# Earlier attention scores for three pairs of heads, and the gates' Strassen unit written out in another order

## The chip, the cores and the metric

The kernel runs on one core of a Trainium2 chip. The metric is device time in microseconds of one execution. The core has a TensorE (PE, matrix products into eight PSUM banks), a VectorE (DVE), a ScalarE (ACT), a GpSimd engine (POOL) and a SyncE queue (SP) that issues DMAs; POOL and ACT can issue DMAs too. Each engine takes its instructions in one fixed order and stops at the first one whose inputs or output buffer are not ready.

## The reference

Two layers, each a half-step feed-forward block, a mixer and another half-step feed-forward block on 256 tokens of width 1024, each followed by a layer norm. The change lies in the mixer:

```
z = x @ w_in;  u, v, q, k, val, gates = split(z)
h_a = chunked_sgu(gelu(u), gelu(v))            # per 128-token chunk, lower triangular
q, k = rope(q), rope(k)
a = softmax(q0 k0) - lam * softmax(q1 k1)      # 8 heads, two score maps each, causal
h_b = rmsnorm(a @ val) * (1 - lam_init)
g = sigmoid(gates + gate_b)                    # [tokens, 2 branches, 1024]
m = g[0] * (h_a @ w_branch[0]) + g[1] * (h_b @ w_branch[1]);  out = m @ w_out
```

All inputs and outputs are float32. Each operand is split into a high and a low part (`whi`/`wlo` for weights), and a product is made as hi·hi + lo·hi + hi·lo.

## The kernel before

TensorE's order is written out by hand: the program's text is the order of the matrix products. The other engines' orders come from a list scheduler at build time, which places each instruction by a priority (`step()` raises it with every chunk of weights) and by its own estimate of when it becomes ready. Two tools bend that. `behind(ins)`, which is `tc.issue_after(ins)`, adds an edge "not before `ins`" to those instructions of its block that stand on the engine of `ins`; instructions of other engines in the block get no edge. `beside(task, delay)` sets a side task aside: a generator whose pieces are put into the text when a counter of product work (`beat`) has advanced by the delay, and whose `yield`s are further delays. A beat is one piece of a gate column's chunk (8 products with `whi` and 8 half-size ones with `wlo`), some 2.8 us.

The mixer of a layer runs in this order on TensorE: values; eight projections for q and k (`rope`, four pairs of heads); four chunks of gate columns and two of u (`gemm_a2`: 16 products with `whi`, L296, then 16 half-size ones with `wlo`, L303), and between these the seven products of the gates' Strassen unit (`gates_by_rows`, products in `product`, L377); the v projection (L284); two more chunks of u; then the branches, of which the first (`branch_rows(1, hb)`, L284) reads `hb`, the result of attention.

Attention is a side task for each pair of heads (`attend`). The four pairs are counted from one here. A pair's way is: scores on TensorE (L1018), maximum and exponentials (DVE L1030, ACT L1032), difference of the two maps (DVE L1041), transposition through POOL (L217), a DMA on SP (L221) and ACT (L1066), the product with the values on TensorE (L1072 and L1074), copy and squares on ACT (L1077, L1082), an inverse root in 16 small steps on POOL (`rsqrt4`, L269 to L277), scaling (ACT L1091), a second transposition (POOL L217, SP L221, DVE L230), and the two parts of `hb` (ACT L1106, DVE L1108).

PSUM has four banks with the tag `main` and four with the tag `side`. A pair's scores take four side banks, its product with the values one. The unit keeps one main bank from its first to its last product, so the gate columns turn round in the other three; a column's bank is free when DVE has added its two halves (`gz`, L306), for which ACT first copies one half (`r`, L304).

The unit's summed weights are made in place: a raw tile is split (`pieces`, ACT L248 and DVE L250), and then POOL adds the next weights to it by an accumulating DMA (`gather`, L354). Before, a gather after a product was itself a side task one beat later (`add_in`).

Of the kernel before, what the change touches and what calls it, by code (L numbers as in the profile page):

```python
# [17 lines left out]
ALU = mybir.AluOpType  # L18
# [19 lines left out]
HC = CH // 2  # L38
# [17 lines left out]
def trunk(ctx, tc, x, xT, w13a, w13b, w2, wb, wqk, wu, wg, wgr, wbr, wbrr, wo, gateb, gatebr, sgug, sgub, sguwT, sgubias, lam, diffg,  # L56
          lng, lnb, lngT, lnbT, cosT, sinT, out):
    nc = tc.nc
    V, A, G, PE = nc.vector, nc.scalar, nc.gpsimd, nc.tensor
# [15 lines left out]
    def name(s):  # L75
        serial[0] += 1
        return f"{s}_{serial[0]}"

    def bank():
        return psum.tile([P, 512], F32, tag="main", name=name("bank"))  # L80
# [4 lines left out]
    def slots(s, n, dtype=F32):  # L85

        return [act.tile([P, 512], dtype, tag="slot", name=name(s)) for _ in range((n + 1) // 2)]
# [22 lines left out]
    def step():  # L110
        chunk[0] += 1
        tc.cur_priority = chunk[0] * STEP
# [12 lines left out]
    def beat(w):  # L125

        clock[0] += w
        for task in list(tasks):
            if task[0] <= clock[0]:
                turn(task)  # L130

    def turn(task):
        try:
            task[0] = clock[0] + next(task[1])
        except StopIteration:
            tasks.remove(task)

    def beside(task, delay):
        tasks.append([clock[0] + delay, task])
# [9 lines left out]
    line = [None, None, False]  # L149

    def inline(eng, ins):
        if line[2]:
            line[eng is V] = ins
        return ins

    def behind(ins):

        return tc.issue_after(ins) if ins is not None else nullcontext()

    def fetch(src, width=CH, raw=None):  # L160

        step()
        if raw is None:
            raw = raw_pool.tile([P, CH], F32, tag="raw", name=name("raw"))
        for g in gate:
            g[0] -= 1
        while len(gate) > 1 and gate[1][0] < 0:
            gate.pop(0)
        with behind(gate[0][1] if gate and gate[0][0] < 0 else None):
            if isinstance(raw, list):  # L170
                for j, v in enumerate(raw):
                    loaded[0] = nc.sync.dma_start(v, src[:, j * HC : (j + 1) * HC]).ins
            else:
                loaded[0] = nc.sync.dma_start(raw[:, :width], src).ins
        return raw
# [70 lines left out]
    def split(hi, lo, src, eng=V, after=(None, None)):  # L246
        with behind(after[0]):
            a = A.activation(hi, src, AF.Copy).ins  # L248
        with behind(after[1]):
            return a, eng.tensor_tensor(out=lo, in0=src, in1=hi.bitcast(F32), op=ALU.subtract).ins  # L250
# [97 lines left out]
    def halved(v):  # L348
        return v if isinstance(v, list) else [v[:, o : o + HC] for o in range(0, CH, HC)]

    def gather(raw, more):
        step()
        for j, v in enumerate(halved(raw)):
            G.dma_start(v, more[:, j * HC : (j + 1) * HC], accum_op=ALU.add)  # L354
        return raw

    def plus(raw, more):
# [2 lines left out]
                inline(V, V.tensor_tensor(out=v, in0=v, in1=m, op=ALU.add).ins)  # L360
        return raw

    def pieces(raw):
        out = []
        for v in halved(raw):
            hi = hi_pool.tile([P, HC], F32R, tag="hi", name=name("whi"))
            lo = lo_pool.tile([P, HC], F32R, tag="lo", name=name("wlo"))
            for eng, ins in zip((A, V), split(hi, lo, v, after=line[:2])):
                inline(eng, ins)
            out.append((hi, lo))  # L370
        return out

    def product(ps, x, w, start, stop):
        for k in range(4):
            hi, lo = (v[:, k % 2 * 512 : k % 2 * 512 + 512] for v in w[k // 2])
            for n, (y, o) in enumerate(((hi, 0), (lo, 0), (hi, 1))):
                PE.matmul(ps, x[o](k), y, start=start and k == n == 0, stop=stop and k == 3 and n == 2,  # L377
                          skip_group_check=True)
            beat(0.25)

    def gemm_seven(src, xh, xl, sums, ln, done):

# [42 lines left out]

        r1 = fetch(w11)
        p1 = pieces(r1)
        r2 = fetch(w12, raw=homes(hi_pool, "hi"))
        product(bx, a11, p1, True, False)
        ln.fold(0, 0, bx, ALU.add, True)  # L430
        between()
        p2 = pieces(fetch(w21))
        plus(r1, r2)
        product(q[0][0], a12, p2, False, False)
        gather(r2, w22)
        r3 = fetch(w22, raw=homes(lo_pool, "lo"))
        between()
# [151 lines left out]
    def bc_load(src, after):  # L589
        t = res.tile([P, D], F32, tag="bc", name=name("bc"), bufs=2)  # L590
        V.tensor_copy(t[:, :1], after)
        spread[0] = G.dma_start(t, src.partition_broadcast(P)).ins
        return t
# [376 lines left out]
    def mixer(l, i, norm):  # L970
# [14 lines left out]
        def rope(src, scale):  # L985

            (_, z), = gemm_a2([src], both, lambda m: slots("z", 2)[0], lambda: t512("r"), scale)
            sw, r = t512("swap"), slots("qk", 2)[0]
            for h in range(2):
                nc.sync.dma_start(sw[h::2, :], z[1 - h :: 2, :])  # L990
            r3, z3, s3 = (v.rearrange("p (j t) -> p j t", j=2) for v in (r, z, sw))
            c, s = (v.unsqueeze(1).to_broadcast([P, 2, T]) for v in (cos_t, sin_t))
            V.tensor_tensor(out=r3, in0=z3, in1=c, op=ALU.mult)
            turned_by[0] = G.tensor_tensor(out=s3, in0=s3, in1=s, op=ALU.mult).ins  # L994

            def rest():
                with behind(added[0]):
                    V.tensor_tensor(out=r, in0=r, in1=sw, op=ALU.add)
                yield 0

            beside(rest(), 1.55)
            return r
# [108 lines left out]
        gates, grow, x_sums = [], [], []  # L1111
# [6 lines left out]
        def gates_by_rows():  # L1118

            x11, x12, x22 = (tuple(lambda k, o=o, t=t, h=h: x_cat[h][:, k, o + t * P : o + (t + 1) * P] for o in (0, T))  # L1120
                             for t, h in ((0, 0), (0, 1), (1, 1)))
            (w11, w21), (w12, w22) = ([wgr[l, br, 0][:, o : o + CH] for o in (0, CH)] for br in range(2))
            grow.extend([slots("gr", 2)[0] for _ in range(NT)] for _ in range(2))
            (g00, g10), (g01, g11) = grow

            def add_in(raw, w):
                def task():
                    gather(raw, w)
                    yield 0
                beside(task(), 1)  # L1130
            bias = [gbias[:, br * 512 : (br + 1) * 512] for br in range(2)]

            def sum_up(out, in0, in1, op, end=False):
                added[0] = V.tensor_tensor(out=out, in0=in0, in1=in1, op=op).ins
                if end:
                    emptied[0] = A.activation(out, out, AF.Tanh, scale=0.5).ins

            bx = bank()
            r1 = fetch(w11)
            product(bx, x11, pieces(r1), True, False)  # L1140
            add_in(r1, w12)
            sum_up(g00, bx, bias[0], ALU.add)
            yield
            bq = bank()
            product(bq, x12, pieces(fetch(w21)), True, True)
            sum_up(g00, bq, g00, ALU.add, True)
            yield
            bz = bank()
            product(bz, x_sums[0], pieces(r1), True, False)
            add_in(r1, w22)  # L1150
            sum_up(g11, bz, bias[1], ALU.add)
            yield
            r3 = fetch(w22)
            product(bz, x_sums[3], pieces(r3), False, True)
            add_in(r3, w12)
            sum_up(g01, bz, bias[1], ALU.add)
            yield
            product(bx, x_sums[1], pieces(r1), False, False)
            add_in(r1, w21)
            sum_up(g01, g01, bx, ALU.subtract, True)  # L1160
            yield
            product(bx, x_sums[2], pieces(r3), False, False)
            sum_up(g11, g11, bx, ALU.subtract, True)
            yield
            product(bx, x22, pieces(r1), False, True)
            sum_up(g10, bx, bias[0], ALU.add, True)
            yield

        beside(sums_of_x(), 3.5)
        for hp in range(HEADS // 2):  # L1170
            qT = rope(wqk[l, hp, 0], HD ** -0.5)
            kT = rope(wqk[l, hp, 1], 1.0)
            beside(attend(hp, qT, kT), 4.5 + 2.1 * hp)
            if hp == 1:
                gbias = bc_load(gatebr[l], qT[:, :1])

# [143 lines left out]
    for l in range(DEPTH):  # L1320
        norm = ffn(l, 0, 0, norm)
        norm = mixer(l, 1, norm)
        norm = ffn(l, 1, 2, norm, last=l == DEPTH - 1)
# [87 lines left out]
```

## Time and profile before

| | |
|---|---|
| median of 3 runs | 1215.14 us (1214.31 to 1221.01) |
| the profiled execution | 1212.97 us, span 1211.3 us |
| PE, DVE, ACT, POOL busy | 1185.6, 1042.6, 839.6, 301.1 us |
| granted TensorE clock, mean | 0.993 |
| the first layer's unit and gate columns | 250.4 to 317.9 us |
| the second layer's | 848.6 to 919.0 us |
| start of the branch that reads `hb` | 352.5 and 954.2 us |

In a timeline row the columns are start, duration, engine, line, operation, output and inputs, shapes, count of instructions merged into the row, and in brackets how long the engine had been idle before it and what ended that. Matrix products overlap: a row's duration is longer than its distance to the next, so rates are read from starts. Line numbers are those of the kernel before.

### The profile page before, as it was taken

What the parts mean: (1) busy time and instruction counts of PE and PEld (TensorE: products, weight loads), DVE (VectorE), ACT (ScalarE), POOL (GpSimd) and SP (SyncE); (2) the same over time, 40 slices, a digit from 0 to 9 for tenths busy, and PEclk for the clock granted to TensorE, in tenths of its full rate; (3) what the DMA queues carried; (4) which work ended last, traced back from release to release, by engine and by line L of the source; (5) the groups of instructions that cost most, each with busy time, mean ns of one, the idle gap of its engine ahead of it and who ended that gap; (6) DMA issues with size and microseconds to landing.
All of it is one profiled execution on the core that took longest, in us unless ns stands there. A gap on an engine that the chain in (4) does not pass through costs nothing.

```text
span 1211.3 us, 16711 instructions
## 1 busy us (share of the span) xinstructions
PE 1185.6 (98%) x5753; PEld 994.5 (82%) x5753; DVE 1042.6 (86%) x1596; ACT 839.6 (69%) x1439; POOL 301.1 (25%) x366
## 2 busy tenths in 40 slices
PE   9999999989989999999999999999799899999998
PEld 8888888878878888888888888888688688888887
DVE  6889989988788989889898889889887799898895
ACT  6787667659854676886667976676698456679770
POOL 1013200255430220071020260003554212201610
PEclk9999999999999999999999999999899999999999
DMA  9867967769864668689578689486797655786880
GB/s 351 271 229 236 303 218 273 239 189 272 280 202 160 194 213 270 194 271 274 184 249 278 206 265 283 135 330 187 203 275 248 217 170 169 248 261 198 271 238 35
DMA packets 131637, 281.40 MB, mean 232 GB/s; under 512 B 89264, under 2 KB 90592, under 8 KB 107744
## 3 DMA queue, kind: packets, MB, share of 16 engines
q1 hardware_dynamic: 121680, 246.57, 61.0%
q0 software_dynamic: 9296, 33.10, 12.2%
q8 instruction: 45, 0.74, 0.2%
q10 hardware_dynamic: 576, 0.66, 0.2%
q14 instruction: 40, 0.33, 0.1%
HBM read 254.35 MB, written 1.05 MB: 211 GB/s over the span
## 4 chain that ended last, share of the span: by engine, by line
PE 75%; DVE 8%; ACT 6%; POOL 4%; DMA 4%; issue 3%; SPq 0%; DVEq 0%; ACTq 0%; POOLq 0%
PE bank L284 37%; PE sbank L377 12%; PE bank L411 9%; PE bank L296 6%; PE sbank L411 3%; PE bank L303 3%; DVE wlo L198 2%; DMA swap<-z 2%; PE bank L531 2%; ACT whi L196 1%; ACT pp L1032 1%; DMA raw<-in_wgr 1%; PE bank L377 1%; DVE wlo L250 1%; DMA on<-onT 1%
## 5 line engine op out<-in xcount | busy, mean ns | idle before, releaser
L198 DVE TENSOR_TENSOR wlo<-raw,whi 128x1024 fp32r<-128x1024 f32 (+1 forms) x330 | 358.7, 1114 | 50.2 <-ACT whi L196 42.8
L196 ACT ACTIVATE whi<-raw 128x1024 fp32r<-128x1024 f32 (+1 forms) x334 | 306.4, 946 | 108.0 <-PE bank L284 34.7
L284 PE MATMUL bank<-whi,x 128*128 128x512 f32 x1096 | 344.6, 389 | 0.0
L284 PEld LDWEIGHTS bank<-whi,x 128*128 128x128 f32 x1096 | 205.8, 188 | 42.6
L284 PE MATMUL bank<-wlo,x 128*128 128x512 f32 x548 | 213.2, 389 | 0.0
L250 DVE TENSOR_TENSOR wlo<-raw,whi 128x1024 fp32r<-128x1024 f32 (+1 forms) x151 | 179.8, 1212 | 29.8 <-ACT whi L248 22.8
L248 ACT ACTIVATE whi<-raw 128x1024 fp32r<-128x1024 f32 (+1 forms) x151 | 149.9, 1012 | 61.5 <-DVE raw L360 31.5
L296 PE MATMUL bank<-x,whi 128*128 128x512 f32 x640 | 157.8, 398 | 12.8 <-DVE z L306 9.2
L296 PEld LDWEIGHTS bank<-x,whi 128*128 128x128 f32 x640 | 119.6, 191 | 40.5 <-DVE z L306 10.2
L284 PEld LDWEIGHTS bank<-wlo,x 128*128 128x128 f32 x548 | 102.9, 188 | 21.3
L230 POOL COPY seven<-seven 128x512 uint16<-128x512 uint16 x16 | 67.0, 4248 | 125.1 <-ACT whi L196 81.1
L303 PEld LDWEIGHTS bank<-x,wlo 128*128 128x128 f32 x640 | 82.1, 193 | 3.2
L303 PE MATMUL bank<-x,wlo 128*128 128x256 f32 x640 | 83.4, 285 | 0.0
L411 PE MATMUL bank<-whi,hhi 128*128 128x512 f32 (+1 forms) x182 | 68.2, 374 | 0.0
L411 PE MATMUL bank<-whi,hlo 128*128 128x512 f32 (+1 forms) x182 | 67.9, 373 | 0.0
L411 PE MATMUL bank<-wlo,hhi 128*128 128x512 f32 (+1 forms) x182 | 67.9, 373 | 0.0
L758 POOL COPY nvia<-ntwo 128x256 uint16<-128x256 uint16 x20 | 10.4, 567 | 158.4 <-DMA ntwo<-nvia 132.6
L994 POOL TENSOR_TENSOR swap<-swap,sin_t 128x512 f32<-128x512 f32 x16 | 23.9, 1493 | 99.2 <-DMA swap<-z 90.3
L1032 ACT ACTIVATE pp<-pp,mx 128x256 f32<-128x256 f32 (+1 forms) x64 | 28.2, 442 | 23.4 <-DVE mx L1030 23.4
L304 ACT ACTIVATE r<-bank 128x256 f32<-128x256 f32 x96 | 33.9, 372 | 13.0 <-PE bank L303 12.7
L377 PE MATMUL sbank<-whi,xhs 128*128 128x512 f32 x128 | 42.0, 389 | 0.0
L411 PEld LDWEIGHTS bank<-whi,hlo 128*128 128x128 f32 x182 | 34.3, 188 | 6.1
(303 smaller groups left out, 2294.6 us busy)
## 6 DMA issues: line engine op xcount, KB each, us to landing
raw<-in_w13b SPq DMA_DIRECT2D x68, 1024.0 KB, 6.0
raw<-in_w SPq DMA_DIRECT2D x32, 1024.0 KB, 6.1
raw<-in_wb SPq DMA_DIRECT2D x16, 1024.0 KB, 7.5
raw<-in_wqk SPq DMA_DIRECT2D x16, 1024.0 KB, 7.0
home<-in_w13b SPq DMA_DIRECT2D x16, 512.0 KB, 6.3
raw<-in_w13a SPq DMA_DIRECT2D x8, 1024.0 KB, 4.9
home<-in_w SPq DMA_DIRECT2D x16, 512.0 KB, 4.5
raw<-in_wg SPq DMA_DIRECT2D x8, 1024.0 KB, 5.7
```

The lines of the kernel that those rows point to most:

```text
L196: inline(A, A.activation(h, r, AF.Copy).ins)
L198: low = eng.tensor_tensor(out=w, in0=r, in1=h.bitcast(F32), op=ALU.subtract).ins
L230: eng.tensor_copy(out=o, in_=i)
L248: a = A.activation(hi, src, AF.Copy).ins
L250: return a, eng.tensor_tensor(out=lo, in0=src, in1=hi.bitcast(F32), op=ALU.subtract).ins
L284: PE.matmul(ps, xx, w, start=start and n == 0, stop=stop and n == 2)
L296: PE.matmul(b[-1], hi[:, k * P : (k + 1) * P], xc(k), start=k == 0, stop=False)
L303: PE.matmul(b[n][:, :T], lo[:, k * P : (k + 1) * P], xc(k)[:, :T], start=False, stop=k == KT - 1)
L304: emptied[0] = A.activation(r[:, s], b[n][:, T:], AF.Copy, scale=scale).ins
L377: PE.matmul(ps, x[o](k), y, start=start and k == n == 0, stop=stop and k == 3 and n == 2, skip_group_check=True)
L411: PE.matmul(q[c][t][:, :n] if o == 0 else more[:, :n], x(k, t), y, start=k == 8 and m == 0 and (c, t) != (1, 0) and not o, stop=k == FT - ...
L1032: A.activation(p[:, s], p[:, s], AF.Exp, bias=mx[:, a], scale=-1.0, accum_out=sums[:, a])
```

## The change

In `gates_by_rows` the gathers are no longer side tasks: each stands in the text right behind the product that it follows, inside `behind(m)`, where `m` is that product's last matrix instruction; and four of the `pieces` calls take `m` too. In `attend`'s delays, 4.5, 6.6, 8.7 and 10.8 beats become 4.5, 6.2, 7.25 and 9.25.

```diff
-    def gather(raw, more):
+    def gather(raw, more, after=None):
         step()
         for j, v in enumerate(halved(raw)):
-            G.dma_start(v, more[:, j * HC : (j + 1) * HC], accum_op=ALU.add)
+            with behind(after):
+                G.dma_start(v, more[:, j * HC : (j + 1) * HC], accum_op=ALU.add)
...
-    def pieces(raw):
+    def pieces(raw, after=None):
...
-            for eng, ins in zip((A, V), split(hi, lo, v, after=line[:2])):
+            for eng, ins in zip((A, V), split(hi, lo, v, after=(after, after) if after else line[:2])):
...
-                PE.matmul(ps, x[o](k), y, start=start and k == n == 0, stop=stop and k == 3 and n == 2,
-                          skip_group_check=True)
+                last = PE.matmul(ps, x[o](k), y, start=start and k == n == 0, stop=stop and k == 3 and n == 2,
+                                 skip_group_check=True)
             beat(0.25)
+        return last.ins
...
-            def add_in(raw, w):
-                def task():
-                    gather(raw, w)
-                    yield 0
-                beside(task(), 1)
...
-            product(bx, x11, pieces(r1), True, False)
-            add_in(r1, w12)
+            m = product(bx, x11, pieces(r1), True, False)
+            gather(r1, w12, m)
...
-            product(bz, x_sums[0], pieces(r1), True, False)
-            add_in(r1, w22)
+            m = product(bz, x_sums[0], pieces(r1, m), True, False)
+            gather(r1, w22, m)
...
-            product(bz, x_sums[3], pieces(r3), False, True)
-            add_in(r3, w12)
+            m = product(bz, x_sums[3], pieces(r3), False, True)
+            gather(r3, w12, m)
...
-            product(bx, x_sums[1], pieces(r1), False, False)
-            add_in(r1, w21)
+            m = product(bx, x_sums[1], pieces(r1, m), False, False)
+            gather(r1, w21, m)
...
-            product(bx, x_sums[2], pieces(r3), False, False)
+            m = product(bx, x_sums[2], pieces(r3, m), False, False)
...
-            product(bx, x22, pieces(r1), False, True)
+            product(bx, x22, pieces(r1, m), False, True)
...
-            beside(attend(hp, qT, kT), 4.5 + 2.1 * hp)
+            beside(attend(hp, qT, kT), (4.5, 6.2, 7.25, 9.25)[hp])
```

Here `m` stands on PE, the gather on POOL, the split on ACT and DVE. With the edits of the unit alone, all five engines' orders read as before, row for row; what moves in the built program moves with the four delays. The first pair keeps its place, and so do the second pair's scores; the third and the fourth move.

TensorE in the first layer, at the first pair's product with the values (`sbank_2619`) and the third pair's scores. Before, the scores stood in the gate column that follows, between its `whi` and `wlo` products:

```order
L377 MATMUL bank_2605<-whi_2612,x_1213 128x512
L296 MATMUL bank_2656<-x_1212,whi_2648 128x512 [waits DVE_49]
L296 MATMUL bank_2656<-x_1212,whi_2648 128x512 x3
L296 MATMUL bank_2656<-x_1213,whi_2648 128x512 x4
L296 MATMUL bank_2690<-x_1212,whi_2652 128x512 [waits DVE_49]
L296 MATMUL bank_2690<-x_1212,whi_2652 128x512 x3
L296 MATMUL bank_2690<-x_1213,whi_2652 128x512 x4
L1018 MATMUL sbank_2703<-qk_2346,qk_2285 128x256
```

and in the change (where L1020 is the line of the scores, L1074 and L1076 those of the values, L378 the unit's):

```order
L1074 MATMUL sbank_2619<-val_1699,d_2278 128x128 [waits Pool_49]
L1076 MATMUL sbank_2619<-val_1699,aT_2279 128x128
L1076 MATMUL sbank_2619<-val_1700,aT_2279 128x128
L1020 MATMUL sbank_2639<-qk_2346,qk_2285 128x256
L1020 MATMUL sbank_2640<-qk_2346,qk_2285 128x256
L1020 MATMUL sbank_2639<-qk_2346,qk_2285 128x256
L1020 MATMUL sbank_2640<-qk_2346,qk_2285 128x256
L1020 MATMUL sbank_2645<-qk_2346,qk_2285 128x128
L1020 MATMUL sbank_2646<-qk_2346,qk_2285 128x128 [waits Activation_49]
L1020 MATMUL sbank_2645<-qk_2346,qk_2285 128x128
L1020 MATMUL sbank_2646<-qk_2346,qk_2285 128x128
L378 MATMUL bank_2605<-whi_2608,x_1213 128x512
```

The scores now stand directly behind the product whose side bank their fourth bank, `sbank_2646`, takes over; the wait on ACT in the sixth row of the scores stood in the same row before. The fourth pair's scores move in the same way, out of the fourth gate column into the unit's fourth product just ahead of it.

ACT in the first layer, from the column copy of the chunk before. Before:

```order
L304 ACTIVATE r_2581<-bank_2566 128x256
L1187 ACTIVATE gate_2512<-gz_2582,gbh 128x256 x2
L1077 ACTIVATE on_2626<-sbank_2619 128x512
L1082 ACTIVATE d_2277,ss_2628<-on_2626 128x128 x4
L248 ACTIVATE whi_2863<-raw_2861 128x1024
L248 ACTIVATE whi_2867<-raw_2861 128x1024
L1136 ACTIVATE gr_2514<-gr_2514 128x512
L196 ACTIVATE whi_2886<-raw_2884 128x1024
L196 ACTIVATE whi_2890<-raw_2884 128x1024
L1032 ACTIVATE pp_2715,sums_2700<-pp_2715,mx_2699 128x256 x2
```

and in the change:

```order
L1183 ACTIVATE gate_2512<-gz_2582,gbh 128x256 x2
L1079 ACTIVATE on_2626<-sbank_2619 128x512
L1084 ACTIVATE d_2277,ss_2628<-on_2626 128x128 x4
L1034 ACTIVATE pp_2651,sums_2636<-pp_2651,mx_2635 128x256 x2
L1034 ACTIVATE pp_2656,sums_2636<-pp_2656,mx_2635 128x256 x2
L1034 ACTIVATE pp_2661,sums_2636<-pp_2661,mx_2635 128x128 x2
L1034 ACTIVATE pp_2666,sums_2636<-pp_2666,mx_2635 128x128 x2
L248 ACTIVATE whi_2865<-raw_2863 128x1024
L1132 ACTIVATE gr_2514<-gr_2514 128x512
L248 ACTIVATE whi_2869<-raw_2863 128x1024
L196 ACTIVATE whi_2926<-raw_2924 128x1024
```

The third pair's eight exponentials go ahead of five instructions; the copy `on_2626<-sbank_2619` keeps its place behind the gate column's two.

DVE in the first layer, at the copy `onT` of the fourth pair, from which `hb_1934` and `hb_1935` are made. Before:

```order
L198 TENSOR_TENSOR wlo_3786<-raw_3783,whi_3785 128x1024
L306 TENSOR_TENSOR u_3556<-bank_3567,r_3605 128x256
L230 COPY onT_3481<-on_3358 128x512 x2
L306 TENSOR_TENSOR u_3556<-bank_3596,r_3605 128x256
L261 TENSOR_SCALAR nwa_3683<-nwy_3680,ve_3671 128x1
L198 TENSOR_TENSOR wlo_3790<-raw_3783,whi_3789 128x1024
L1108 SCALAR_TENSOR_TENSOR hb_1934<-onT_3481,dgs,hb_1934 128x256
```

and in the change:

```order
L198 TENSOR_TENSOR wlo_3570<-raw_3563,whi_3569 128x1024
L198 TENSOR_TENSOR wlo_3640<-raw_3637,whi_3639 128x1024
L230 COPY onT_3445<-on_3316 128x512 x2
L198 TENSOR_TENSOR wlo_3644<-raw_3637,whi_3643 128x1024
L1208 BN_STATS vst_3273<-vg_3271 128x6
```

The copy stands 32 rows earlier, ahead of the norm of v, and the two `hb` rows 13 rows earlier, right behind the first half of the third chunk of u.

More of the change, by code (lines that the diff above doesn't have):

```diff
@@ L1144, in gates_by_rows @@
             bq = bank()
-            product(bq, x12, pieces(fetch(w21)), True, True)
+            m = product(bq, x12, pieces(fetch(w21)), True, True)
             sum_up(g00, bq, g00, ALU.add, True)
```

## The prediction

> **What bounds the kernel now.** The page first, since it says which engine a gain has to come from.
>
> ```profile
> span 1211.3 us, 16711 instructions
> PE 1185.6 (98%) x5753; PEld 994.5 (82%) x5753; DVE 1042.6 (86%) x1596; ACT 839.6 (69%) x1439; POOL 301.1 (25%) x366
> ```
>
> TensorE is busy 98% of the span, so a change that adds no product can only win or lose at TensorE's waits. The view of waits on that engine lists them (total, times, longest):
>
> ```profile
> PE bank L296 <- DVE z L306: 9.2, 3, 5.7
> PE bank L284 <- ACT hb L1106: 6.1, 2, 3.0
> PE bank L296 <- DVE gz L306: 3.6, 6, 1.0
> PE bank L284 <- DVE hb L1108: 1.1, 2, 0.7
> PE bank L284 <- DVE u L306: 1.0, 2, 0.8
> ```
>
> The first stands before anything the change moves. The `hb` waits are the fourth pair of heads coming late to the branch; the `gz` waits lie between the unit's products. Their price is more than the idle time, as TensorE's timeline shows, first layer, then second:
>
> ```profile
> 341.02 3.79 PE L296 MATMUL bank<-x,whi 128*128 128x512 f32 x16
> 344.65 2.08 PE L303 MATMUL bank<-x,wlo 128*128 128x256 f32 x16
> ...
> 356.47 0.39 PE L284 MATMUL bank<-whi,hb 128*128 128x512 f32 x1
> 359.90 0.50 PE L284 MATMUL bank<-whi,hb 128*128 128x512 f32 x1 [3.04 <-ACT hb L1106]
> ...
> 367.95 1.05 PE L1244 MATMUL sbank<-wsT,vg 128*128 128x128 f32 x8
> ...
> 958.17 0.39 PE L284 MATMUL bank<-whi,hb 128*128 128x512 f32 x1
> ...
> 969.20 1.05 PE L1244 MATMUL sbank<-wsT,vg 128*128 128x128 f32 x8
> ```
>
> Sixteen undisturbed products go from 341.02 to 344.65, 0.227 us each. From the last product before the wait to L1244 lie 25 such steps (one, six with the fourth pair's `hb`, eighteen more), worth 5.67 us. They took 11.48 and 11.03, so the two `hb` waits cost 5.8 and 5.4 us, 11.2 in all, slow clock behind them included.
>
> Why is `hb` late? PE, ACT, SP and DVE in the first layer, and the landing times of the transposing DMA:
>
> ```profile
> 317.91 0.39 PE L284 MATMUL bank<-whi,x 128*128 128x512 f32 x1
> ...
> 327.43 0.38 PE L1072 MATMUL sbank<-val,d 128*128 128x128 f32 x2
> ```
> ```profile
> 339.42 1.28 ACT L1091 ACTIVATE on<-on,nwy 128x128 f32<-128x128 f32 x4 [3.64 <-POOL nwy L277]
> ```
> ```profile
> 341.95 1.24 SPq L221 DMA_TRANSPOSE on<-onT x1
> ```
> ```profile
> 341.68 2.46 DVE L198 TENSOR_TENSOR wlo<-raw,whi 128x1024 fp32r<-128x1024 f32 x2 [4.64 <-ACT whi L196]
> ...
> 352.01 0.42 DVE L306 TENSOR_TENSOR u<-bank,r 128x256 f32<-128x256 f32 x1
> ...
> 358.47 0.78 DVE L230 COPY onT<-on 128x512 uint16<-128x512 uint16 x2
> ```
> ```profile
> DMA to landing us min/median/max: 4.6/6.6/10.2
> ```
>
> The block lands near 348.6 (341.95 + 6.6), at the latest 352.2, but DVE comes to it at 358.47 without having waited: it stood in DVE's queue. So two things matter, when the fourth pair's chain ends and where its rows stand on DVE.
>
> **The change part by part.** *The unit's edits* cost and bring nothing. Their order edges would tie POOL, ACT and DVE to an instruction of PE, and such an edge binds only an instruction of the same engine; the order of all engines is the same with and without them.
>
> *The fourth pair, sooner.* Its product with the values stood behind 42 products of the v projection ((327.43 - 317.91) / 0.227) and now stands behind 18, which is 5.4 us less, while TensorE will be some 2 us late there (next part): 3.4 us sooner. If the rest of the chain follows, the scaling comes at 336.0, the DMA at 338.5, the block at 345.1, at the latest 348.8. The DVE copy now stands between the two splits of 341.68, so DVE waits there from 342.9 to 345.1, and all behind it comes 2 to 3 us later: `u` at 352.01 becomes 354 to 355, which is when TensorE, 2 us late, first needs it (that cover is thin: each us more is a us of waiting), and the `hb` rows follow `u` directly, four to five us before TensorE wants them. In the second layer the copy stands behind `u` and holds nothing up. Both `hb` waits go: **11.2 us**.
>
> *The third pair, sooner.* Here the change adds a wait. TensorE around the place, first layer:
>
> ```profile
> 265.49 0.47 PE L377 MATMUL bank<-whi,x 128*128 128x512 f32 x1
> ...
> 268.19 3.92 PE L296 MATMUL bank<-x,whi 128*128 128x512 f32 x16 [0.39 <-DVE gz L306]
> 272.05 1.58 PE L1018 MATMUL sbank<-qk,qk 64*128 64x256 f32 x16
> 273.55 2.18 PE L303 MATMUL bank<-x,wlo 128*128 128x256 f32 x16
> ...
> 278.09 0.39 PE L377 MATMUL bank<-whi,xhs 128*128 128x512 f32 x1
> 279.49 3.96 PE L296 MATMUL bank<-x,whi 128*128 128x512 f32 x16 [1.00 <-DVE gz L306]
> ```
>
> The scores took 272.05 to 273.55. They will begin at 265.49, and their sixth row takes the side bank of the first pair's values, which ACT has to copy out first. Five of eight rows (four of 256 columns, one of 128) are three quarters of 1.50 us, so TensorE stops at 265.49 + 1.13 = 266.6. ACT's copy and what it stands behind:
>
> ```profile
> 264.85 2.96 DVE L250 TENSOR_TENSOR wlo<-raw,whi 128x1024 fp32r<-128x1024 f32 x2
> 267.73 0.74 DVE L306 TENSOR_TENSOR gz<-bank,r 128x256 f32<-128x256 f32 x2
> ```
> ```profile
> 268.18 0.91 ACT L1187 ACTIVATE gate<-gz,gbh 128x256 f32<-128x256 f32 x2 [3.02 <-DVE gz L306]
> 268.99 0.58 ACT L1077 ACTIVATE on<-sbank 128x512 f32<-128x512 f32 x1
> ```
>
> The copy follows two gate rows, these follow `gz`, and `gz` follows two weight splits on DVE. None of it depends on a product later than 265.49, so the copy ends at 269.57 as before, and TensorE stands for 269.6 - 266.6 = 3.0 us. Behind it in TensorE's queue wait the rest of the unit's second product and the whole gate column. In the second layer the same rows are these:
>
> ```profile
> 866.60 0.47 PE L377 MATMUL bank<-whi,x 128*128 128x512 f32 x1
> ```
> ```profile
> 870.11 0.57 ACT L1077 ACTIVATE on<-sbank 128x512 f32<-128x512 f32 x1
> ```
>
> 870.7 - (866.6 + 1.1) = 3.0 again: **6.0 us** of standing.
>
> Then the clock. After a stand of the same length the profile shows this:
>
> ```profile
> 258.12 3.25 PE L296 MATMUL bank<-x,whi 128*128 128x512 f32 x8 [3.02 <-DVE z L306]
> 261.17 2.53 PE L303 MATMUL bank<-x,wlo 128*128 128x256 f32 x16
> 263.54 0.40 PE L377 MATMUL bank<-whi,x 128*128 128x512 f32 x1
> ```
>
> Eight products and sixteen half-size ones took 263.54 - 258.12 = 5.42 us; at the rates of 341.02 to 346.56 they take 1.81 + 1.91. The stand cost 1.7 us more in slow products, and the two `hb` waits (11.2, less 6.1 + 1.1 of idle) 2.0 each. I take 1.7 each, **3.4 us**; the bounds are 0 and 2.1.
>
> The Trainium skill (TensorE: Matmul & The Clock Gate, section "What's actually happening") says that the clock is halved after at least one idle window of about 3.4 us, the windows running freely. By that rule a stand of 3.0 us holds no whole window and costs no slow products, and the sum below would be 3.4 us better; the row after 3.02 us of idle speaks against it.
>
> *What TensorE's lateness takes away.* It comes 4 us later to 279.49, while ACT's two copies `r` stay where they were:
>
> ```profile
> 278.61 0.63 ACT L304 ACTIVATE r<-bank 128x256 f32<-128x256 f32 x2
> ```
>
> In the new order ACT does the eight exponentials from 270.8 to 274.6 (3.5 us, as long as before), four splits and a gate row (4.4 us), and these copies at 279.0; DVE, through the difference of the maps and three splits, gives `gz` at 280.6. TensorE arrives near 282, so it does not wait. In the same way the waits at 268.19 and before the fourth column go, and TensorE, 2 us late, no longer waits for `u`. All six `gz` waits and both `u` waits: 3.6 + 1.0 of idle, and each loses 0.17 us more between starts than it shows as idle (279.49 - 278.09 - 0.23 = 1.17 for 1.00), so 4.6 + 1.3 = **5.9 us**; bounds 0 and 5.9.
>
> *The gather that moves.* On POOL the third gather now stands behind the third pair's transposition copies. This is the one that landed slowest, in the chain of waits:
>
> ```profile
> 278.72 12.20 DMA raw<-in_wgr
> ```
>
> I put its issue 2 us later, so landing near 293. By the same walk through ACT's order (exponentials of the fourth pair from 290.7 to 294.2) ACT comes to its split at 294.2, and the third pair's transposed block is ready at 303.2 for a product that TensorE reaches at 305. So a landing up to 296 costs nothing.
>
> Sum against the profiled execution's own 1212.97: -11.2 - 5.9 + 6.0 + 3.4 = **-7.7**, 1205.3. That execution lies 2.2 below the median of the runs shown; against 1215.14 it is **1207.5**.
>
> **The rivals.** *The clock stays up*: a stand of 3.0 us may be just too short to lower it. Then the 3.4 us are not lost, 1204. For it: no shorter stand in the profile shows slow products. Against: the two quoted are only 0.02 and 0.04 us longer. The page named above would have it so.
>
> *What is lost stays lost*: the `gz` waits move along with TensorE, since ACT and DVE are as full as before and get the exponentials ahead of the splits, and the clock costs 2.1 each. Then 11.2 - 6.0 - 4.2 = 1 us is gained, 1214. For it: ACT's copies come at 279.0, no sooner than 278.6. Against: TensorE is nearly 4 us later there.
>
> *Slower: the late gather.* Between 280 and 300 the transfers of the unit, the weights and the transpositions fall together. If the third gather lands after 296 instead of 293, ACT stands at its split, in order, and with it the evacuation of the fourth column and the third pair's transposed block; TensorE then stops before that pair's values. At 301 it is a stop of 5 us with 1.7 of slow clock in each layer, 13.4 in all, and 5.7 us slower than before: 1221. For it: it was the slowest landing already. Against: it has to land 8 us later than at the worst rate seen.
>
> **How the numbers follow.** A measurement of this kernel tells 0.5%, about 6 us, from no change. Forecast, 1204 to 1211 around 1207.5: 0.50. The clock stays up: 0.12. Lost stays lost: 0.22. Late gather: 0.16, of which half passes 0.5%. The bound for faster, 1209, cuts the forecast's own range at about four fifths: faster 0.40 + 0.12 = 0.52; slower 0.10 with what I do not see; the same 0.38. The range runs from 1202.5 (all waits gone and a clock that stays up) to 1216, between the second and the third rival.
>
> **What would show it.** The view of TensorE's waits should hold no `hb` and hardly any `gz`, and a new line: sbank L1020, from ACT, two times, 3.0 each. The product after it should run at half rate for some 4 us. DVE's L230 should be early and wait for its DMA in the first layer. I am wrong if L1020 has no wait (another bank was taken over), if `hb` is still waited for, or if TensorE stops at L1074 for the third pair.

## The result, and the profile after

The changed kernel took 1209.83 us (median of ten executions, 1205.67 to 1212.84) where the kernel before took 1220.96 beside it. The ratio of the means is 0.9917, 95% interval 0.989 to 0.9945. Measured a second time it was 0.9951 (0.9925 to 0.9977), with medians of 1214.26 and 1219.44. So the change makes the kernel faster, by 0.8% and by 0.5%. The forecast was 1207.5 us, 0.6% less than the median shown then. The profiled execution took 1206.0 us, 7.0 less than the one of before (1212.97); the forecast for it was 7.7.

The page's first lines and TensorE's waits (total, times, longest) in the changed kernel:

```profile
span 1204.3 us, 16725 instructions
PE 1181.6 (98%) x5753; PEld 994.8 (83%) x5753; DVE 1040.9 (86%) x1596; ACT 841.0 (70%) x1439; POOL 299.4 (25%) x366
...
PE bank L296 <- DVE z L306: 8.5, 3, 5.7
PE sbank L1020 <- ACT on L1079: 5.4, 2, 2.8
PE bank L284 <- DVE u L306: 4.1, 1, 4.1
```

Every `hb`, `gz` and small `u` wait of the list of before is gone. The second line is the wait foretold at the third pair's scores. The third was not foretold: one stand of 4.1 us for `u` (the branch's products need the bank out of which DVE makes `u`). TensorE's timeline shows where they lie:

```profile
263.27 0.38 PE L1074 MATMUL sbank<-val,d 128*128 128x128 f32 x2
...
264.69 1.35 PE L1020 MATMUL sbank<-qk,qk 64*128 64x256 f32 x10
268.62 0.71 PE L1020 MATMUL sbank<-qk,qk 64*128 64x128 f32 x6 [2.58 <-ACT on L1079]
...
275.08 2.08 PE L303 MATMUL bank<-x,wlo 128*128 128x256 f32 x16
...
349.60 2.07 PE L303 MATMUL bank<-x,wlo 128*128 128x256 f32 x16
355.81 0.53 PE L284 MATMUL bank<-whi,hb 128*128 128x512 f32 x1 [4.14 <-DVE u L306]
...
367.08 1.05 PE L1240 MATMUL sbank<-wsT,vg 128*128 128x128 f32 x8
...
864.01 0.38 PE L1074 MATMUL sbank<-val,d 128*128 128x128 f32 x2
...
869.61 0.71 PE L1020 MATMUL sbank<-qk,qk 64*128 64x128 f32 x6 [2.82 <-ACT on L1079]
...
952.70 0.40 PE L284 MATMUL bank<-whi,hb 128*128 128x512 f32 x1
...
962.24 1.05 PE L1240 MATMUL sbank<-wsT,vg 128*128 128x128 f32 x8
```

These rows give a ledger by stage. I take as a **stage** the stretch from the first pair's product with the values (L1074; L1072 before) to the first row of L1240 (L1244 before): all that the change touches lies in it. Its start before, in the two layers:

```profile
264.24 0.38 PE L1072 MATMUL sbank<-val,d 128*128 128x128 f32 x2
...
865.35 0.38 PE L1072 MATMUL sbank<-val,d 128*128 128x128 f32 x2
```

With the ends 367.95 and 969.20 shown in the prediction, the stage took 103.71 and 103.85 us before, and now 367.08 - 263.27 = 103.81 and 962.24 - 864.01 = 98.23. **The first layer gained nothing, the second 5.6 us.** Another 1.0 us was gained ahead of the first layer's stage and 0.5 between the two, where the change moves nothing.

Why nothing in the first layer? From 355.81 to 367.08 TensorE makes the same 42 products that take 962.24 - 952.70 = 9.54 us in the second layer. Here they took 11.27, and before them TensorE stood from 351.51 (349.60 and the 1.91 us of L303) to 355.81. So the wait for `u` cost 4.30 + 1.73 = 6.0 us, as much as the `hb` wait it stands in for (5.8). DVE and SP of that place:

```profile
345.42 0.80 DVE L230 COPY onT<-on 128x512 uint16<-128x512 uint16 x2 [4.26 <-DMA on<-onT]
...
355.34 0.41 DVE L306 TENSOR_TENSOR u<-bank,r 128x256 f32<-128x256 f32 x1
```
```profile
337.25 1.23 SPq L221 DMA_TRANSPOSE on<-onT x1
```

DVE comes to the fourth pair's copy 4.26 us before its block has landed and stands there; `u` follows 9.9 us later. There had been no slack to begin with, for in the kernel before TensorE already waited for `u` at this place:

```profile
352.48 0.50 PE L284 MATMUL bank<-whi,hb 128*128 128x512 f32 x1 [0.20 <-DVE u L306]
```

### The profile page after: what moved, and what is told of

Its sections match the earlier page's. It is cut to its first block, busy times and chain, and to the rows that moved or that the text cites. A ratio compares the mean times of both kernels' runs of the same rounds, so it can differ in the third digit from the quotient of the medians.

```text
span 1204.3 us, 16725 instructions
## 1 busy us (share of the span) xinstructions
PE 1181.6 (98%) x5753; PEld 994.8 (83%) x5753; DVE 1040.9 (86%) x1596; ACT 841.0 (70%) x1439; POOL 299.4 (25%) x366
## 4 chain that ended last, share of the span: by engine, by line
PE 85%; DVE 6%; ACT 4%; DMA 2%; issue 2%; POOL 2%; SPq 0%; DVEq 0%; POOLq 0%; ACTq 0%
PE bank L284 40%; PE sbank L378 12%; PE bank L413 10%; PE bank L296 9%; PE bank L303 4%; PE sbank L413 3%; PE bank L378 3%; PE bank L533 2%; DVE wlo L198 1%; DMA swap<-z 1%; ACT whi L196 1%; DMA on<-onT 1%; DVE qk L1000 1%; DVE wlo L250 1%; POOL swap L996 1%
## 5 line engine op out<-in xcount | busy, mean ns | idle before, releaser
L284 PE MATMUL bank<-whi,x 128*128 128x512 f32 x1096 | 345.0, 390 | 0.0
L284 PEld LDWEIGHTS bank<-whi,x 128*128 128x128 f32 x1096 | 205.8, 188 | 42.9 <-DVE u L306 0.3
L284 PE MATMUL bank<-wlo,x 128*128 128x512 f32 x548 | 213.4, 389 | 0.0
L284 PEld LDWEIGHTS bank<-wlo,x 128*128 128x128 f32 x548 | 102.9, 188 | 21.1
L230 POOL COPY seven<-seven 128x512 uint16<-128x512 uint16 x16 | 66.8, 4231 | 125.5 <-ACT whi L196 81.1
L303 PEld LDWEIGHTS bank<-x,wlo 128*128 128x128 f32 x640 | 81.7, 192 | 2.7
L303 PE MATMUL bank<-x,wlo 128*128 128x256 f32 x640 | 82.6, 283 | 0.0
L996 POOL TENSOR_TENSOR swap<-swap,sin_t 128x512 f32<-128x512 f32 x16 | 23.7, 1483 | 97.4 <-DMA swap<-z 81.6
L378 PE MATMUL sbank<-whi,xhs 128*128 128x512 f32 x128 | 42.0, 389 | 0.0
```

The lines of the kernel that those rows point to most:

```text
L230: eng.tensor_copy(out=o, in_=i)
L284: PE.matmul(ps, xx, w, start=start and n == 0, stop=stop and n == 2)
L303: PE.matmul(b[n][:, :T], lo[:, k * P : (k + 1) * P], xc(k)[:, :T], start=False, stop=k == KT - 1)
L378: last = PE.matmul(ps, x[o](k), y, start=start and k == n == 0, stop=stop and k == 3 and n == 2, skip_group_check=True)
```

## The experiments

One execution's profile is one draw. So beside the ratio to the kernel before (its runs are shared by the kernels measured together), I give the two stages of the profiled execution.

**The unit's edits alone**: the changed kernel with the old delays.

```diff
-            beside(attend(hp, qT, kT), (4.5, 6.2, 7.25, 9.25)[hp])
+            beside(attend(hp, qT, kT), 4.5 + 2.1 * hp)
```

> The unit's edits alone (adding transfers and parts tied behind block products, no task around them); the delays of the kernel before. Theory A, as predicted: the edits move no instruction, so 1.000 of the kernel before (0.998 to 1.002), and TensorE's waits show the two hb waits (3.0 us each) and the six gz waits as before. Theory B: the ties act on the chip although the order is the same (a transfer issued later, a split held back); then some of the 0.8% found for the whole change is here, 0.992 to 0.997, and the gz waits or the gather's landing move.

Measured: 0.9985 (0.9949 to 1.0022). No gain can be told, as theory A has it; the interval reaches into theory B's range, but the second layer's stage, 103.80 for 103.85, shows no effect. However, the profiled execution took 1221.28 us, and its first stage 111.13 instead of 103.71, with the same order of instructions. ACT's timeline and the unit's adding transfers show why:

```profile
305.60 1.06 ACT L248 ACTIVATE whi<-raw 128x1024 fp32r<-128x1024 f32 x1 [5.88 <-DMA raw<-in_wgr]
310.42 1.06 ACT L248 ACTIVATE whi<-raw 128x1024 fp32r<-128x1024 f32 x1 [2.96 <-DMA raw<-in_wgr]
...
DMA to landing us min/median/max: 5.4/8.7/21.9
```

The slowest of the adding transfers (all that L355 issues) took 21.9 us to land. In the two profiled executions compared above the slowest took 12.2 (before) and 11.8 (after). A late adding transfer, which the prediction held for a possible consequence of the change, also strikes an order that it has not touched.

**The third pair alone (with the second pair's 6.2), and the fourth alone:**

```diff
-            beside(attend(hp, qT, kT), (4.5, 6.2, 7.25, 9.25)[hp])
+            beside(attend(hp, qT, kT), (4.5, 6.2, 7.25, 10.8)[hp])
```
```diff
-            beside(attend(hp, qT, kT), (4.5, 6.2, 7.25, 9.25)[hp])
+            beside(attend(hp, qT, kT), (4.5, 6.6, 8.7, 9.25)[hp])
```

> Delays 4.5, 6.2, 7.25, 10.8: the third pair's scores early, the fourth pair's where they were. Theory A (the ledger of the two traces): the stand at the third pair's scores (2.6 to 3.0 us in each layer) takes back what the gz and u waits (2.9 us) give, so 1.000 (0.997 to 1.002); both hb waits are still there. Theory B (the stand is pure loss, the gz waits come back behind it): two times 3 to 5 us slower, 1.005 to 1.008. Theory C (third pair's move is worth its 5.9 us of waits and the stand costs little): 0.995.

> Delays 4.5, 6.6, 8.7, 9.25: the fourth pair's scores early, the third pair's where they were. Theory A: the second layer loses its hb wait (5.4 us), the first swaps it for a wait for u behind the early copy (about 0), no stand at the scores, the gz waits stay: -5 to -6 us, 0.9955 (0.993 to 0.997). Theory B (my prediction's sum for this part): both hb waits go and nothing comes in their place, -11, 0.991. Theory C (the fourth pair can't go ahead of the third: TensorE stops at its values, or ACT's exponentials of both pairs collide): no gain, 0.998 to 1.003, and a new wait at L1074.

Measured: third alone 0.9967 (0.9929 to 1.0005), stages 103.61 and 103.34; fourth alone 0.9938 (0.9904 to 0.9971), stages 107.82 and 102.92. TensorE's rows, third alone first:

```profile
270.42 1.22 PE L1020 MATMUL sbank<-qk,qk 64*128 64x128 f32 x6 [2.70 <-ACT on L1079]
...
362.01 0.50 PE L284 MATMUL bank<-whi,hb 128*128 128x512 f32 x1 [1.58 <-ACT hb L1108]
```
```profile
359.00 0.80 PE L284 MATMUL bank<-whi,hb 128*128 128x512 f32 x1 [3.96 <-DVE u L306]
...
916.70 0.46 PE L1074 MATMUL sbank<-val,d 128*128 128x128 f32 x2 [2.67 <-ACT d L1068]
```

In the stages the third alone fits theory A: the stand and what it replaces come out even, with 2.9 and 1.6 us of slow products behind the two stands in this execution. The ratio's interval also holds theory C's 0.995. Since TensorE is later, the first layer's `hb` wait shrinks from 3.04 to 1.58. The fourth alone has theory A's `u` wait in the first layer and no `hb` wait, and also theory C's stop at L1074; its slowest adding transfer took 20.6 us. Its profiled execution (1216.07) is among its slowest, so the stages say little about its usual gain; by the ratios, whose intervals overlap, the fourth pair brings most of the gain.

**The copy behind `u`**: the fourth pair's copy L230 a little later, so that in the first layer it stands between the two `u` rows. TensorE's order is the same.

```diff
-            yield 1.8
+            yield 1.8 if hp < 3 else 2.1
             with behind(added[0]):
                 joined(on, onT, V)
```

> The whole change, but in the first layer DVE's copy of the fourth pair's transposed block (L230) stands between the two u instead of between two weight splits. Theory A: the 4.3 us that DVE waits at that copy are what makes u late, and the stand of 4.1 us at L284 and the 1.7 us of slow products behind it go: 6 us less than the whole change, 0.987 of the kernel before (0.984 to 0.990). Theory B: u is late for another reason (its weights, ACT's copies, PE's lateness), and the copy only fills the gap: as the whole change, 0.992. Theory C: the copy now comes so late that hb is waited for again, 3 us and more: 0.993 to 0.996.

> The whole change with DVE's copy L230 of the fourth pair behind the first u of the first layer, again, since four executions left it unclear. Theory A: no stand at L284 for u in the first layer, 4.2 us of standing and 1.7 of slow products less than the whole change: 0.987 of the kernel before (0.985 to 0.989). Theory B (what comes before eats it up, or hb is then late): 0.990 to 0.993.

Measured: 0.9875 (0.9788 to 0.9961) with four executions, then 0.9903 (0.9866 to 0.994) with six. In the second profile DVE and TensorE stand so:

```profile
349.60 0.42 DVE L306 TENSOR_TENSOR u<-bank,r 128x256 f32<-128x256 f32 x1
349.94 0.78 DVE L230 COPY onT<-on 128x512 uint16<-128x512 uint16 x2
```
```profile
351.81 2.08 PE L303 MATMUL bank<-x,wlo 128*128 128x256 f32 x16
353.72 0.40 PE L284 MATMUL bank<-whi,hb 128*128 128x512 f32 x1
```

`u` comes before TensorE needs it, nothing stands at L284 and `hb` is in time. That DVE's wait at the copy made `u` late is shown: the edit moves that copy, a few DVE rows near it and one row `r` on ACT, TensorE's order stays, and the stand is gone in both profiles. (The rows `r` had come at 345.20 and 347.12 in the changed kernel, 8 us and more before `u`, so ACT was not what `u` waited for.) In the second profile the first stage is 99.67, 4.1 less than in the changed kernel, although here 1.6 us of slow products lie behind its stand at L1020, and there none. Its second stage, 102.63, is 4.4 longer than there, 3.0 of it slow products behind the stand and 1.5 waits for `u`. In the first profile (1212.0, stages 103.97 and 100.54) a late adding transfer hides the gain, and TensorE stands for `u` at another place. ACT, then TensorE:

```profile
308.64 1.06 ACT L248 ACTIVATE whi<-raw 128x1024 fp32r<-128x1024 f32 x1 [1.95 <-DMA raw<-in_wgr]
```
```profile
317.93 2.75 PE L296 MATMUL bank<-x,whi 128*128 128x512 f32 x8 [3.04 <-DVE u L306]
```

The ratio's gain is not that sure: 0.9903 overlaps the changed kernel's 0.9951, measured beside it.

**The copy of the first pair's values ahead of the gate rows.** This takes the stand at L1020 away without moving a TensorE instruction: the first column's two gate rows are held back in the text until ACT's copy `on` has been written.

```diff
+                    def tanh(s=s, k=k, b=b, g=gt[c]):
+                        A.activation(g[:, s], b[:, s], AF.Tanh, scale=0.5, bias=gbh[:, l, br, k : k + 1])
+                    held_gates.append(tanh) if br == c == 0 else tanh()
...
             A.activation(on, b, AF.Copy)
+            while held_gates:
+                held_gates.pop(0)()
```

> The whole change, but ACT copies the first pair's values (on) ahead of the two gate rows of the first column instead of behind them, so the third pair's scores find their side bank free: the stand at L1020 goes in both layers. Theory A (my prediction's reason for the lost gz waits: they go because TensorE comes late): TensorE comes 2.6 to 2.8 us sooner to the unit's third product, whose splits DVE gives at 276.8 and not sooner, so a wait of 2 us for gz or wlo comes back there in each layer; net 0.3 to 1 us a layer, as the whole change, 0.990 to 0.992 of the kernel before. Theory B (the stand is pure loss, the gz waits had gone for the new order's sake): 2.7 us a layer and the slow products behind some of them, 6 to 8 us less, 0.985 to 0.987, and no gz wait.

Measured: 0.9921 (0.9895 to 0.9946), as the whole change; stages 104.79 and 98.30. TensorE:

```profile
280.11 3.92 PE L296 MATMUL bank<-x,whi 128*128 128x512 f32 x16 [1.59 <-DVE gz L306]
...
358.62 0.80 PE L284 MATMUL bank<-whi,hb 128*128 128x512 f32 x1 [5.59 <-DVE u L306]
...
882.14 3.92 PE L296 MATMUL bank<-x,whi 128*128 128x512 f32 x16 [2.00 <-DVE gz L306]
```

Theory A. TensorE comes sooner and the `gz` wait is back, 1.6 and 2.0 us; what is left over in the first layer is stood out for `u`, 5.6 us for 4.1.

**Both edits together**, early copy and copy behind `u`:

> Both edits: on copied ahead of the gate rows (no stand at L1020) and L230 behind u. Theory A: in the first layer the early copy of on gave nothing because TensorE stopped for u all the longer (5.6 for 4.1 us); with that stand gone the gz waits that come back (1.6 to 2.0 us a layer) still leave about 1 us a layer, and no clock is lost behind the stands: 0.984 to 0.986 of the kernel before, 2 to 3 us under the copy behind u alone. Theory B: the waits for gz, wlo and u after it take all of it: as the copy behind u alone, 0.987.

Measured: 0.9856 (0.9828 to 0.9885), 1199.57 to 1203.35 us in six executions, stages 97.49 and 97.20. This beats both kernels. The early copy alone had shown nothing, since the wait for `u` swallowed what it gave. TensorE's waits:

```profile
PE bank L296 <- DVE z L306: 10.5, 3, 6.3
PE bank L296 <- DVE gz L306: 2.7, 2, 1.6
```

**The stand filled with work.** With the copy behind `u`, the third pair's first four score rows are written six times over:

```diff
-                for j in range(2):
+                for j in range(12 if hp == 2 and t else 2):
+                    j %= 2
```

> The changed kernel once more, on the chip of the next three, to compare with. Where the profiled execution of it had both stands at L1020 (2.6 and 2.8 us) without slow products, the other kernels with the same stands showed slow products behind five of six; so a profile of an execution near the median should have slow products behind at least one of the two and lie some 2 to 4 us over 1204.3. If it has none again, the slow products belong to the other kernels' orders and not to the execution.

> L230 behind u, and the stand at L1020 filled with work: the first four score rows of the third pair are computed six times over (20 more products of 64 by 256, 2.7 us, same values in the same place), so TensorE does not stand there but reaches the sixth row no sooner. Theory A (slow products come from standing): none behind L1020, nine products of the unit in 2.0 us in both layers, 1.7 to 2 us a stand less than the copy behind u alone on the mean, 0.984 to 0.986 of the kernel before. Theory B (they come from something else in the execution, such as the z stand 10 us ahead, or the rows of half height don't count as work): slow products there as in the others, and the time of the copy behind u alone, 0.987.

The filled stand: 0.9896 (0.986 to 0.9932) and 1203.84 us, where the copy behind `u` alone had 0.9903 and 1206.32; six executions each, so no gain can be told. Its profile, and below it that of the copy behind `u` (the second one, second layer):

```profile
266.42 5.90 PE L1021 MATMUL sbank<-qk,qk 64*128 64x256 f32 x56
272.24 0.50 PE L378 MATMUL bank<-whi,x 128*128 128x512 f32 x1
...
274.42 3.79 PE L296 MATMUL bank<-x,whi 128*128 128x512 f32 x16
278.04 2.08 PE L303 MATMUL bank<-x,wlo 128*128 128x256 f32 x16
```
```profile
865.20 1.22 PE L1020 MATMUL sbank<-qk,qk 64*128 64x128 f32 x6 [2.35 <-ACT on L1079]
866.34 0.79 PE L378 MATMUL bank<-whi,x 128*128 128x512 f32 x1
...
870.35 4.44 PE L296 MATMUL bank<-x,whi 128*128 128x512 f32 x16
874.62 1.60 PE L303 MATMUL bank<-x,wlo 128*128 128x256 f32 x12
```

From the unit's first product to L303 it is 5.80 us with the filled stand (in its second layer too) against 8.28. No slow products in either layer: theory A in the trace. The fill was 1.2 us too long, though: from the first score to the first product it took 5.82, in the changed kernel 269.26 - 264.69 = 4.57. The time forecast, 0.984 to 0.986, was missed; with the fill too long, that is no evidence against theory A.

The changed kernel, measured again, had its profile at 1217.67 us, one of its slowest. Slow products lay behind one of its two stands at L1020, as expected, but they explain 1.6 us; most came from elsewhere. ACT and TensorE in the second layer:

```profile
902.10 1.06 ACT L248 ACTIVATE whi<-raw 128x1024 fp32r<-128x1024 f32 x1 [1.60 <-DMA raw<-in_wgr]
911.21 0.78 ACT L1068 ACTIVATE aT<-d 128x512 uint16<-128x512 uint16 x1 [3.41 <-DMA d<-aT]
```
```profile
914.20 0.77 PE L1074 MATMUL sbank<-val,d 128*128 128x128 f32 x2 [3.24 <-ACT d L1068]
```

A late adding transfer, a late transposition, and TensorE stopped before the third pair's values: the rival of the late gather, in that execution.

**Without the fourth adding transfer**, in the kernel before and in the changed one:

```diff
-            add_in(r1, w21)
```
```diff
-            gather(r1, w21, m)
```

> The kernel before without the unit's fourth adding transfer in each layer (the last product is then made from a sum that lacks one block of the weights; everything else is done). Theory A: in some executions that transfer lands 18 us after its issue instead of 8 to 10 (as in the run of the unit's edits alone, where ACT waited 5.9 and 3.0 us for it and the layer took 7 us more), and these executions are the upper half of the kernel's runs; without it the runs lie at 1212 to 1217, median 1214 to 1215, 0.995 of the kernel before. Theory B: the spread has other causes (other transfers, the clock behind the z waits); the median is the kernel before's, 0.999 to 1.000, and runs over 1219 remain.

> The whole change without the unit's fourth adding transfer in each layer (the last product lacks one block of the weights; everything else is done). Theory A: the change is worth 7 to 8 us where that transfer is in time and 10 over all runs because it is late in more runs of the kernel before than of the changed one; so this lies 7 to 8 us under the kernel before without that transfer, at 1205 to 1208, 0.988 to 0.990 of the kernel before, 2 to 3 us under the whole change. Theory B (the late transfer has no part in it): as the whole change, 0.992, and 10 us under the kernel before without that transfer.

Measured: the kernel before without it 0.9963 (0.9931 to 0.9994), 1215.34 us, all ten executions between 1213.21 and 1218.42, where 10 of the 25 of the full kernel beside it were over 1219. So that transfer makes the upper part of the kernel's times: theory A. Whether only by its own landing, or also by holding up other transfers, these runs do not separate. The changed kernel without it took 1210.03 us (0.9933, 0.9905 to 0.996), not the 1205 to 1208 expected. Here the forecast fell: beside the changed kernel's first measurement (1209.83) leaving the transfer out gave nothing that can be seen; beside the second (1214.26, on another chip) it stays open. Without it the change is worth 1215.34 - 1210.03 = 5.3 us.

**The fourth pair early, the third where it was, and the copy behind `u`:**

> Delays 4.5, 6.6, 8.7, 9.25 (the third pair's scores where they were before the change, so no stand at L1020) and L230 behind u. It asks what moving the third pair adds once both new stands are gone. Theory A (the third pair's place is worth little by itself: its gz waits come back when the stand goes): as both edits together or 1 to 2 us behind, 0.985 to 0.988 of the kernel before. Theory B (the fourth pair needs the third out of its way: with the third late, both pairs' exponentials and transpositions crowd, TensorE stops at L1074 for it as in the run of the fourth pair alone, 2.7 us in one layer): 4 to 8 us behind both edits together, 0.989 to 0.992.

Measured: 0.9864 (0.9823 to 0.9905), 1206.97 us. The ratio says theory A, but the kernel before ran high beside it (1223.28 us, against 1217.6 to 1221.0 in the other comparisons), and in microseconds its fastest execution, 1205.37, is slower than the slowest of both edits together, 1203.35. The stages, 98.89 and 101.68, are 1.4 and 4.5 us longer than those, by waits for `gz`, `u` and at L1074 of under 1.1 us each. What the third pair's place adds stays open between 0 and 6 us.

## Why the prediction was right, and where it was wrong

**The unit's edits cost and bring nothing**: no effect was measured (0.9985), and the second layer's stage, which no late transfer struck, took 103.80 us for 103.85.

**Both `hb` waits go, 11.2 us**: right. In the second layer, where nothing took their place, the stage is 5.6 us shorter.

**Two stands of 3.0 us at the third pair's scores**: right in place and releaser (2.58 and 2.82 us idle).

**The `gz` and `u` waits go because TensorE is late, 5.9 us**: right, reason included; take the lateness away and they come back at 1.6 and 2.0 us. The rival by which they stay is out.

**Slow clock behind the stands, 1.7 us each**: absent in the profiled execution, so there the rival that the clock stays up held. Over six profiles (the change twice, the third pair alone, the copy behind `u` twice, the change without the fourth transfer) there are twelve such stands. From the sixth score row to L303 the shortest time is 275.08 - 268.62 = 6.46 us; the longest, 874.62 - 865.20 = 9.42. Nine of the twelve show slow products, 1.6 to 3.0 us, and the mean loss of the twelve is 1.7. So the term was right on the mean, and its upper bound, 2.1, too low. My grounds for the odds were wrong, though: I had set the stand's 3.0 us against the 3.02 us of a row with slow products, and the length of the stand does not decide (last section).

**"That cover is thin: each us more is a us of waiting"** is the step that failed. I priced the early copy of the first layer at nothing and it cost 6.0 us. The landing (345.1 forecast, about 345.4 seen) and `u` (354 to 355, seen 355.34) were nearly right. Wrong was when TensorE needs it: I set that at the same 354 to 355, by a lateness of 2 us, and it came at 351.5. The stand at L1020 only replaced the waits it swallowed, so TensorE was hardly late. Nor would slow clock have saved it: in the run without the fourth transfer, with slow products behind its stand, TensorE stood 3.9 us for `u` all the same, since the fourth pair's chain starts from TensorE and came later too. There was no cover at all.

The lower end of the stated range does not follow from the terms either: with all waits gone and a clock that stays up they give 1204.0, not 1202.5.

With the terms as measured the sum is -11.2 - 5.9 + 5.4 + 6.0 = -5.7, and the two stages changed by +0.10 - 5.62 = -5.5. That the total came out near -7.7 owes something to luck: a missing loss (slow clock, 3.4) against a loss unforeseen (`u`, 6.0), and 1.5 us gained where nothing was changed.

**The late gather**: its mechanism is real, with TensorE stopped before the third pair's values in one execution, but it needs no change of the order; with the order of before it struck as well (the unit's edits alone), and it makes the upper part of that kernel's times. I had held a profile's slowest landing for the worst to be expected.

## What to carry to other kernels

When a chain is moved earlier, look at where its last row lands in an in-order queue: a row that waits for a transfer at the head of a queue costs every row behind it, and moving that one row behind the next one that TensorE needs took the stand away. A stand that goes is worth only what the next wait leaves, so two edits of which neither shows a sure gain can be worth a per cent together. Compare stage by stage between two rows that both kernels have, and take more than one profile before a difference of a few microseconds is explained.

## What was unexpected in the hardware

The slowest of the unit's adding transfers landed 11.8 us after its issue in one execution of the changed kernel and 23.7 us in another, with the median hardly moved (first and second profile, all transfers of L355):

```profile
DMA to landing us min/median/max: 5.5/8.1/11.8
```
```profile
DMA to landing us min/median/max: 5.5/9.0/23.7
```

Why one execution has such a landing and the next has none was not found.

Slow products followed stands of 2.10 to 2.92 us idle in some executions and not in others, of the same length: 2.58 and 2.82 us without them, 2.57 and 2.82 with. In one execution 1.54 us of idle was enough, with the first slow product 1.2 us after the restart. The Trainium skill (TensorE: Matmul & The Clock Gate, section "What's actually happening") has the clock halved after at least one idle window of about 3.4 us, the windows running free. That the outcome changes between executions of one order fits windows that run free; that stands well under 3.4 us are enough does not fit the rule as it is worded, and here the rows decide.

The traces also show what sorts the stands. In every trace kept here the granted clock is halved and raised again only at points of a grid of 3.41 us; in the changed kernel's first execution it is half from 257.16 to 260.57, from 356.14 to 359.56 and from 854.49 to 861.32. Below are stretches cut along that grid (length, TensorE's busy time, granted clock, DMA share, GB/s): the stand of 1.54 us in the first execution of the copy behind `u`, then the one of 2.58 us in the changed kernel.

```profile
268.00:271.39 3.39, 1.85 (x15) 1.00 0.63 91
271.41:274.80 3.39, 3.39 (x10) 0.50 0.98 186
```
```profile
263.99:267.39 3.40, 2.06 (x17) 1.00 0.38 92
267.41:270.80 3.39, 2.18 (x13) 1.00 0.69 116
270.82:274.20 3.38, 3.38 (x17) 1.00 1.01 221
```

The shorter stand lies in one stretch, 1.54 us of idle, and the next stretch runs at half clock. The longer one is split into 1.35 and 1.23 us, and the clock stays up. All twelve stands sort in this way: the nine with slow products have 1.54 to 2.10 us of idle in one stretch, the three without have 1.47 at most. The order of instructions does not fix where a stand falls on the grid, so whether it costs slow products is a matter of chance. The bound is not one number for every place: elsewhere in these traces stretches with up to 1.84 us of idle were followed by full clock, and from 1.91 us on none was. What else enters was not tested.
